# Moving x and the outputs of an eight-expert MLP into the weights' DMA queue

## The chip, the cores and the metric

The kernel runs on one core of a Trainium2 chip. A core has TensorE (PE) for matmuls with its weight load (PEld), VectorE (DVE), ScalarE (ACT), GpSimd (POOL) and SyncE (SP). Any of the last three may issue DMAs; all DMAs of the core run on the same 16 DMA engines. A DMA issued by POOL can change the type on its way, here fp32 in DRAM to bf16 on chip. Time is device microseconds (us), from the median of the runs; the profile is of one execution.

## What is computed

Eight experts, each a two-layer MLP with a ReLU between, and each on its own 256 rows:

```python
    n_experts, capacity, hidden, expert_hidden = 8, 256, 512, 2048
def reference(x, w1, w2):
    h = np.matmul(x, w1)
    h = np.maximum(h, 0)
    return np.matmul(h, w2).astype(np.float32)
```

All arrays are fp32 in DRAM. Each w1[e] and each w2[e] has 4.19 MB, each x[e] and each output 0.524 MB: 71.3 MB are read and 4.19 MB written. Inside, the kernel works in bf16 with fp32 sums.

## The kernel before

The kernel walks through the experts 0 to 7. Per expert it needs four things.

- **x.** `load_x` (line 57, issued by SP) brings x[e] as fp32 into one of three buffers. `prepare` casts it to bf16 on VectorE (line 88), transposes it in eight 128x128 blocks on TensorE (line 92) and copies the result from PSUM (line 94).
- **w1.** `load_w1` (line 62, POOL) is one DMA that casts 4.19 MB of fp32 to 2.1 MB of bf16; four buffers. Each of the 128 partitions gets one long row.
- **w2.** `load_w2` (line 75, POOL) does the same for w2, but in pieces for the last two experts: `PIECES` cuts the 16 k-rows of expert 6 into 8, 4, 4 and those of expert 7 into 4, 4, 3, 2, 1, 1, 1. Whole w2 have three buffers, pieces their own.
- **The matmuls.** `layer1` makes 64 matmuls (line 108) in eight pairs, each pair followed by a ReLU on ScalarE (line 115) into `hT`. `layer2` makes 32 (line 131); VectorE copies each half of the result to `out_sb` (line 142), except that ScalarE copies the last half of expert 7 (line 140).

POOL's DMAs run from one list, w1 and w2 of each expert in turn, except that w1 of expert 7 stands before w2 of expert 6. `advance` takes two loads from it per expert. Inside `manual_schedule`, PE and POOL execute in the order in which the code is written. On TensorE that is: first layer of e, transposes of e+1, second layer of e; at the end the first layer of 7 comes before the second layers of 6 and 7.

A load waits until its buffer is free (for TensorE), and, from the ninth POOL DMA on, also for the landing of the POOL DMA eight before it. DMAs of one queue are moved in the order of their issue.

Outputs of experts 0 to 4 are stored by SP (line 149). Those of experts 5 and 6 (`DEFER`) are stored by POOL after all weights (line 176). Expert 7's two halves are stored by SP and ACT as soon as each is copied (line 145).

Of the kernel before, what the change touches and what calls it, by code (L numbers as in the profile page):

```python
# [8 lines left out]

FP32 = mybir.dt.float32  # L10
BF16 = mybir.dt.bfloat16

@with_exitstack
def kernel(
    ctx: ExitStack,
    tc: tile.TileContext,  # L20
    x: bass.AP,
    w1: bass.AP,
    w2: bass.AP,
    out: bass.AP,
):
    nc = tc.nc
    P = 128
    E, C, H = x.shape
    F = w1.shape[2]
    MC = C // P  # L30
    K1 = H // P
    K2 = F // P

    x_v = x.rearrange("e (p mo) k -> e p (mo k)", mo=MC)
    out_v = out.rearrange("e (p mo) k -> e p (mo k)", mo=MC)
    w1_v = w1.rearrange("e (p ko) n -> e p (ko n)", ko=K1)
    w2_v = w2.rearrange("e (p j) n -> e p (j n)", p=P)

    const = ctx.enter_context(tc.tile_pool(name="const", bufs=1))
    x_pool = ctx.enter_context(tc.tile_pool(name="x_pool", bufs=3))  # L40
    xb_pool = ctx.enter_context(tc.tile_pool(name="xb_pool", bufs=2))
    xT_pool = ctx.enter_context(tc.tile_pool(name="xT_pool", bufs=2))
    w1_pool = ctx.enter_context(tc.tile_pool(name="w1_pool", bufs=4))
    w2_pool = ctx.enter_context(tc.tile_pool(name="w2_pool", bufs=4))
    hT_pool = ctx.enter_context(tc.tile_pool(name="hT_pool", bufs=2))
    out_pool = ctx.enter_context(tc.tile_pool(name="out_pool", bufs=4))
    psum_t = ctx.enter_context(tc.tile_pool(name="psum_t", bufs=1, space=bass.MemoryType.PSUM))
    psum_h = ctx.enter_context(tc.tile_pool(name="psum_h", bufs=3, space=bass.MemoryType.PSUM))
    psum_o = ctx.enter_context(tc.tile_pool(name="psum_o", bufs=4, space=bass.MemoryType.PSUM))

    identity = const.tile([P, P], BF16, name="identity")

    xs, w1s, w2s = {}, {}, {}

    def load_x(e):
        t = x_pool.tile([P, MC * H], FP32, name="x_sb")
        nc.sync.dma_start(t[:], x_v[e])
        xs[e] = t

    def load_w1(e):  # L60
        t = w1_pool.tile([P, K1 * F], BF16, name="w1_sb")
        nc.gpsimd.dma_start(t[:], w1_v[e])  # L62
        w1s[e] = t

    PIECES = {E - 2: [8, 4, 4], E - 1: [4, 4, 3, 2, 1, 1, 1]}
    BUFS = {16: 3, 8: 1, 4: 4, 3: 1, 2: 1, 1: 3}

    DEFER = (E - 3, E - 2)

    def load_w2(e):  # L70
        w2s[e] = []
        k = 0
        for n in PIECES.get(e, [16]):
            c = w2_pool.tile([P, n * H], BF16, name=f"w2_{n}", bufs=BUFS[n])
            nc.gpsimd.dma_start(c[:], w2_v[e, :, k * H:(k + n) * H])  # L75
            for q in range(n):
                w2s[e].append(c[:, q * H:(q + 1) * H])
            k += n


    weights = []
    for e in range(E):
        weights += [(load_w1, e), (load_w2, e)]
    weights[-3], weights[-2] = weights[-2], weights[-3]

    def prepare(e):
        xb = xb_pool.tile([P, MC, P, K1], BF16, name="xb")
        nc.vector.tensor_copy(xb[:].rearrange("p m q k -> p (m q k)"), xs[e][:])  # L88
        xt_ps = psum_t.tile([P, K1, MC, P], BF16, name="xt_ps")
        for ko in range(K1):  # L90
            for mo in range(MC):
                nc.tensor.transpose(xt_ps[:, ko, mo, :], xb[:, mo, :, ko], identity[:])  # L92
        xT = xT_pool.tile([P, K1, C], BF16, name="xT")
        nc.vector.tensor_copy(  # L94
            xT[:].rearrange("p k c -> p (k c)"),
            xt_ps[:].rearrange("p k m q -> p (k m q)"),
        )
        return xT

    def layer1(e, xT):  # L100
        w1_r = w1s[e][:].rearrange("p (ko q j) -> p ko q j", ko=K1, j=K2)
        hT = hT_pool.tile([P, K2, C], BF16, name="hT")
        for pr in range(K2 // 2):
            h_ps = psum_h.tile([P, 2, C], FP32, name="h_ps")
            for s in range(2):
                j = pr * 2 + s
                for ko in range(K1):
                    nc.tensor.matmul(  # L108
                        h_ps[:, s, :],
                        w1_r[:, ko, :, j],  # L110
                        xT[:, ko, :],
                        start=(ko == 0),
                        stop=(ko == K1 - 1),
                    )
            nc.scalar.activation(  # L115
                hT[:, pr * 2:pr * 2 + 2, :].rearrange("p a c -> p (a c)"),
                h_ps[:].rearrange("p a c -> p (a c)"),
                mybir.ActivationFunctionType.Relu,
            )
        return hT  # L120

    def layer2(e, hT):
        last = e == E - 1
        out_sb = out_pool.tile([P, MC, H], FP32, name="out_sb")
        o_ps = [psum_o.tile([P, H], FP32, name="o_ps") for _ in range(MC)]
        if e in PIECES:
            order = [(k, m) for k in range(K2) for m in range(MC)]
        else:
            order = [(k, m) for m in range(MC) for k in range(K2)]
        for k, m in order:  # L130
            nc.tensor.matmul(  # L131
                o_ps[m][:],
                hT[:, k, m * P:(m + 1) * P],
                w2s[e][k],
                start=(k == 0),
                stop=(k == K2 - 1),
            )
            if k == K2 - 1:
                if last and m == 1:
                    nc.scalar.copy(out_sb[:, m, :], o_ps[m][:])  # L140
                else:
                    nc.vector.tensor_copy(out_sb[:, m, :], o_ps[m][:])  # L142
                if last:
                    eng = nc.scalar if m == 1 else nc.sync
                    eng.dma_start(out_v[e, :, m * H:(m + 1) * H], out_sb[:, m, :])
        if e in DEFER:
            deferred.append((e, out_sb))
        elif not last:
            nc.sync.dma_start(out_v[e], out_sb[:].rearrange("p m h -> p (m h)"))

    deferred = []

    def advance(n):
        for _ in range(n):
            if weights:
                f, e = weights.pop(0)
                f(e)

    load_x(0)
    load_x(1)  # L160
    advance(1)
    make_identity(nc, identity)
    advance(1)
    with tc.manual_schedule(engines={mybir.EngineType.PE, mybir.EngineType.Pool}):
        xT = prepare(0)
        for e in range(E - 1):
            advance(2)
            if e + 2 < E:
                load_x(e + 2)
            hT = layer1(e, xT)  # L170
            xT = prepare(e + 1)
            if e == E - 2:
                hT_last = layer1(E - 1, xT)
            layer2(e, hT)
        for e, o in deferred:
            nc.gpsimd.dma_start(out_v[e], o[:].rearrange("p m h -> p (m h)"))  # L176
        layer2(E - 1, hT_last)


# [1 line left out]
_INS = ['x', 'w1', 'w2']  # L181
_OUTS = [((8, 256, 512), 'float32')]
# [25 lines left out]
```

## Time and profile before

| What | Value |
|---|---|
| Median of 8 runs | 184.11 us (183.69 to 185.18) |
| The profiled execution's own time | 184.12 us |
| Its span, first to last instruction | 182.3 us |
| TensorE matmuls, busy | 131.3 us (72%) |
| VectorE, ScalarE, busy | 21.0 us, 40.1 us |
| Matmuls of `layer1`, `layer2` | 71.3 us (311 ns each), 55.9 us (379 ns each) |
| Casts of x on VectorE | 5.6 us (8 x 701 ns) |
| w1 loads, issue to landing | 64.7 us median |
| x loads by SP, issue to landing | 27.8 us median |
| Stores by SP of experts 0 to 4, issue to landing | 25.4 us median |
| The two stores by POOL, issue to landing | 8.5 us median |
| Second of these issued | at 172.65 us |
| Expert 7's halves issued by SP and ACT | at 178.70 and 178.81 us |
| The same, issue to landing | 2.0 and 2.6 us |
| First POOL load issued | at 1.25 us |
| First matmul of `layer1` | at 16.45 us |

How to read it: the chain of work that ended last is followed back from the end, and gives for each step when it started, how long it took and what it was. A row of waits names who waited, for whom, the sum in us, how often and the longest. The slices cut the span in 40 equal parts; a digit is the busy share in tenths, 9 for 90% and more. A queue's row has its packets, the MB that they wrote and the time that they took as a share of 16 engines; packets can overlap, so shares may sum to more than 100%. A view by windows gives the same for any stretch of time.

### The profile page before, as it was taken

Reading aid. Unit: us, or ns where it says so; the run is one execution under the profiler, and the core shown is the slowest. Engines: PE = TensorE matmul, PEld = TensorE weight load, DVE = VectorE, ACT = ScalarE, POOL = GpSimd, SP = SyncE. Lnnn points to the kernel's source line nnn. Section 1 sums busy time; section 2 is a strip of 40 time slices with the busy share of each in tenths; the row PEclk is TensorE's granted clock in tenths of the full one; section 3 lists DMA queues with packets and bytes.
Section 4 is the critical chain, followed back from the end, with each engine's and each line's share of the span. In section 5 each row is a group of like instructions: output and inputs, shape, how many; then the busy total and the mean of one; then the engine's idle time right before and its main releaser. Section 6 shows DMA issues by size and latency. Waiting matters only on the chain.

```text
span 182.3 us, 1886 instructions
## 1 busy us (share of the span) xinstructions
PE 131.3 (72%) x824; PEld 92.3 (51%) x832; DVE 21.0 (12%) x31; ACT 40.1 (22%) x66; POOL 15.1 (8%) x32
## 2 busy tenths in 40 slices
PE   0203979539896496946989389595978679899990
PEld 0103874228842395415864069342874259794440
DVE  0301013100121002110031100211010200100201
ACT  2000550003600054001440026200450016461001
POOL 7300000200002000020030010101001010112100
PEclk9999999966999789995799969998799969999998
DMA  5999999999999999999999999999999998999993
GB/s 220 272 226 216 258 245 216 245 257 216 227 276 215 220 279 219 217 272 230 215 265 238 216 261 230 208 223 230 216 242 233 230 230 182 223 202 216 206 296 138
DMA packets 5911, 42.05 MB, mean 231 GB/s; under 512 B 656, under 2 KB 1040, under 8 KB 3984
## 3 DMA queue, kind: packets, MB, share of 16 engines
q0 software_dynamic: 3744, 34.60, 88.6%
q1 hardware_dynamic: 2016, 7.08, 10.3%
q10 hardware_dynamic: 144, 0.26, 0.4%
q8 instruction: 6, 0.10, 0.2%
q14 instruction: 1, 0.01, 0.0%
HBM read 71.30 MB, written 4.19 MB: 414 GB/s over the span
## 4 chain that ended last, share of the span: by engine, by line
PE 57%; DMA 26%; another core or an unknown queue 12%; POOL 1%; issue 1%; DVE 0%; ACT 0%; POOLq 0%
PE h_ps L108 29%; PE o_ps L131 27%; DMA w<-in_w_dram 26%; PE xt_ps L92 1%; POOL w_sb L62 1%; DVE xT L94 0%; ACT out_sb L140 0%; POOL w L75 0%; POOL identity masks.py:199 0%; POOL identity masks.py:197 0%; POOLq masks.py:199 0%; POOLq L192 0%
## 5 line engine op out<-in xcount | busy, mean ns | idle before, releaser
L108 PE MATMUL h_ps<-xT,w_sb 128*128 128x256 bf16 x512 | 71.3, 311 | 33.3 <-DMA w_sb<-in_w_dram 32.4
L108 PEld LDWEIGHTS <-w_sb 128*128 128x128 bf16 x512 | 63.2, 150 | 42.8 <-DMA w_sb<-in_w_dram 36.6
L115 ACT ACTIVATE hT<-h_ps 128x512 bf16<-128x512 f32 x64 | 38.2, 597 | 124.7 <-PE h_ps L108 124.7
L131 PE MATMUL o_ps<-w,hT 128*128 128x512 bf16 x248 | 55.9, 379 | 8.7 <-DMA w<-in_w_dram 8.3
L131 PEld LDWEIGHTS <-hT 128*128 128x128 bf16 x256 | 25.0, 98 | 37.6 <-issue 9.0
L75 POOL DMA_DIRECT2D w<-in_w_dram x16 | 8.5, 532 | 136.9 <-PE o_ps L131 71.7
L142 DVE COPY out_sb<-o_ps 128x512 f32<-128x512 f32 x15 | 10.3, 691 | 58.0 <-PE o_ps L131 58.0
L94 DVE COPY xT<-xt_ps 128x1024 bf16<-128x1024 bf16 x8 | 5.5, 692 | 84.1 <-PE xt_ps L92 84.1
L92 PE MATMUL xt_ps<-identity,xb 128*128 128x128 bf16 x64 | 5.3, 230 | 4.9 <-DVE xb L88 4.9
L88 DVE CAST xb<-x_sb 128x1024 bf16<-128x1024 f32 x8 | 5.6, 701 | 15.5 <-DMA x_sb<-in_x_dram 15.5
L92 PEld LDWEIGHTS <-xb 128*128 128x128 bf16 x64 | 4.7, 117 | 4.9 <-DVE xb L88 4.9
L62 POOL DMA_DIRECT2D w_sb<-in_w_dram x8 | 5.0, 630 | 13.5 <-PE h_ps L108 12.7
L140 ACT COPY out_sb<-o_ps 128x512 f32<-128x512 f32 x1 | 0.6, 586 | 13.2 <-PE o_ps L131 13.2
L176 POOL DMA_DIRECT2D out_dram<-out_sb x2 | 1.1, 536 | 7.3 <-DVE out_sb L142 5.1
L115 ACT ACT_TABLE_LOAD x1 | 1.3, 1283 | 0.7 <-PEq L192 0.7
masks.py:199 POOL TENSOR_SCALAR_AFFINE_SELECT identity<-identity 128x128 bf16<-128x128 bf16 x1 | 0.3, 315 | 0.1
masks.py:197 POOL MEMSET identity<- 128x128 bf16 x1 | 0.2, 224 | 0.0
L192 POOL MEMSET const-float32-0.0<- 128x1 f32 x1 | 0.1, 99 | 0.2 <-issue 0.2
L192 POOL MEMSET const-bfloat16-1.0<- 128x1 bf16 x1 | 0.1, 102 | 0.0
L192 POOL MEMSET const-uint8-127<- 128x1 uint8 x1 | 0.1, 102 | 0.0
L192 POOL MEMSET const-float32-1.0<- 128x1 f32 x1 | 0.1, 99 | 0.0
## 6 DMA issues: line engine op xcount, KB each, us to landing
w_sb<-in_w_dram POOLq DMA_DIRECT2D x8, 2048.0 KB, 64.7
w<-in_w_dram POOLq DMA_DIRECT2D x6, 2048.0 KB, 58.1
x_sb<-in_x_dram SPq DMA_DIRECT2D x8, 512.0 KB, 27.8
out_dram<-out_sb SPq DMA_DIRECT2D x5, 512.0 KB, 25.4
w<-in_w_dram POOLq DMA_DIRECT2D x4, 512.0 KB, 56.1
w<-in_w_dram POOLq DMA_DIRECT2D x1, 1024.0 KB, 67.3
out_dram<-out_sb POOLq DMA_DIRECT2D x2, 512.0 KB, 8.5
w<-in_w_dram POOLq DMA_DIRECT2D x1, 384.0 KB, 35.7
```

The source lines that it names most:

```text
L62: nc.gpsimd.dma_start(t[:], w1_v[e])
L75: nc.gpsimd.dma_start(c[:], w2_v[e, :, k * H:(k + n) * H])
L88: nc.vector.tensor_copy(xb[:].rearrange("p m q k -> p (m q k)"), xs[e][:])
L92: nc.tensor.transpose(xt_ps[:, ko, mo, :], xb[:, mo, :, ko], identity[:])
L94: nc.vector.tensor_copy(xT[:].rearrange("p k c -> p (k c)"), xt_ps[:].rearrange("p k m q -> p (k m q)"),)
L108: nc.tensor.matmul(h_ps[:, s, :], w1_r[:, ko, :, j], xT[:, ko, :], start=(ko == 0), stop=(ko == K1 - 1),)
L115: nc.scalar.activation(hT[:, pr * 2:pr * 2 + 2, :].rearrange("p a c -> p (a c)"), h_ps[:].rearrange("p a c -> p (a c)"), mybir.ActivationF ...
L131: nc.tensor.matmul(o_ps[m][:], hT[:, k, m * P:(m + 1) * P], w2s[e][k], start=(k == 0), stop=(k == K2 - 1),)
L140: nc.scalar.copy(out_sb[:, m, :], o_ps[m][:])
L142: nc.vector.tensor_copy(out_sb[:, m, :], o_ps[m][:])
L176: nc.gpsimd.dma_start(out_v[e], o[:].rearrange("p m h -> p (m h)"))
L192: nc = _bacc.Bacc("TRN2", target_bir_lowering=False, num_devices=1)
```

## The change

x of experts 2 to 7 is no longer loaded by SP and cast by VectorE. POOL loads it in pairs, (2, 3), (4, 5) and (6, 7), with the cast in the DMA, each pair placed in the weights' list before w1 of expert 1, 3 and 5. x of experts 0 and 1 is loaded and cast as before. Every load of w2 now fills a part of one whole buffer out of four. Expert 6's w2 comes in pieces of 8, 8 and expert 7's in 4, 4, 4, 2, 2.

Outputs are collected in one tile for each group: (0, 1, 2), (3, 4, 5, 6) and (7). POOL stores the first group in one DMA, which stands in its queue between w1 of expert 7 and w2 of expert 6, and the second group in one DMA after the last piece of w2. Expert 7's two halves are stored as before. The identity for the transposes is made twice.

The order of POOL's DMAs is then: w1 of 0, w2 of 0, x of 2 and 3, w1 and w2 of 1, w1 and w2 of 2, x of 4 and 5, w1 and w2 of 3 and of 4, x of 6 and 7, w1 and w2 of 5, w1 of 6, w1 of 7, outputs 0 to 2, w2 of 6 (2 pieces), w2 of 7 (5 pieces), outputs 3 to 6. The rule of eight counts all of these. TensorE's order is the one of before. SP keeps x of 0 and 1 and one half of expert 7.

```diff
-    x_pool = ctx.enter_context(tc.tile_pool(name="x_pool", bufs=3))
+    x_pool = ctx.enter_context(tc.tile_pool(name="x_pool", bufs=2))
-    out_pool = ctx.enter_context(tc.tile_pool(name="out_pool", bufs=4))
+    out_pool = ctx.enter_context(tc.tile_pool(name="out_pool", bufs=1))
...
+    PIECES = {E - 2: [8, 8], E - 1: [4, 4, 4, 2, 2]}
+    GROUPS = [(0, 1, 2), (3, 4, 5, 6), (7,)]
+    GROUP = {e: g for g in GROUPS for e in g}
+    DEFER = GROUPS[-2]
+    X_GROUPS = [(2, 3), (4, 5), (6, 7)]
...
+    def load_x(g):
+        t = xb_pool.tile([P, 2, MC, P, K1], BF16, name="xb2")
+        nc.gpsimd.dma_start(
+            t[:].rearrange("p e m q k -> p e (m q k)"), xg_v[:, g[0]:g[0] + 2, :]
+        )
+        for i, e in enumerate(g):
+            xbs[e] = t[:, i]
...
     def load_w2(e):
-        w2s[e] = []
+        w2s[e] = t = w2_pool.tile([P, K2 * H], BF16, name="w2_sb")
         k = 0
-        for n in PIECES.get(e, [16]):
-            c = w2_pool.tile([P, n * H], BF16, name=f"w2_{n}", bufs=BUFS[n])
-            nc.gpsimd.dma_start(c[:], w2_v[e, :, k * H:(k + n) * H])
...
+        for n in PIECES.get(e, [K2]):
+            nc.gpsimd.dma_start(t[:, k * H:(k + n) * H], w2_v[e, :, k * H:(k + n) * H])
             k += n
+    def store(g):
+        nc.gpsimd.dma_start(
+            og_v[:, g[0]:g[-1] + 1, :], outs[g][:].rearrange("p e m h -> p e (m h)")
+        )
...
     def prepare(e):
-        xb = xb_pool.tile([P, MC, P, K1], BF16, name="xb")
-        nc.vector.tensor_copy(xb[:].rearrange("p m q k -> p (m q k)"), xs[e][:])
+        xb = xbs[e]
...
     def layer2(e, hT):
-        out_sb = out_pool.tile([P, MC, H], FP32, name="out_sb")
+        g = GROUP[e]
+        if e == g[0]:
+            outs[g] = out_pool.tile([P, len(g), MC, H], FP32, name=f"out_sb{g[0]}")
+        out_sb = outs[g][:, e - g[0]]
...
-        if e in DEFER:
-            deferred.append((e, out_sb))
-        elif not last:
-            nc.sync.dma_start(out_v[e], out_sb[:].rearrange("p m h -> p (m h)"))
...
+    load_x_first(0)
+    load_x_first(1)
     with tc.manual_schedule(engines={mybir.EngineType.PE, mybir.EngineType.Pool}):
+        f, e = loads.pop(0)
+        f(e)
+        make_identity(nc, identity)
+        f, e = loads.pop(0)
+        f(e)
+        make_identity(nc, identity)
+        issue([(load_w2, 0), (load_x, X_GROUPS[0]), (load_w1, 1), (load_w2, 1), (load_w1, 2)])
         xT = prepare(0)
         for e in range(E - 1):
-            advance(2)
-            if e + 2 < E:
-                load_x(e + 2)
+            issue(
+                [(load_w2, e + 2), (load_w1, e + 3), (load_w1, E - 1), (load_w2, e + 1)]
+                + [(load_x, g) for g in X_GROUPS if g[0] <= e + 4]
+            )
+            for g in GROUPS[:-2]:
+                if g[-1] == e - 1:
+                    store(g)
             hT = layer1(e, xT)
             xT = prepare(e + 1)
             if e == E - 2:
                 hT_last = layer1(E - 1, xT)
             layer2(e, hT)
-        for e, o in deferred:
-            nc.gpsimd.dma_start(out_v[e], o[:].rearrange("p m h -> p (m h)"))
+        store(DEFER)
         layer2(E - 1, hT_last)
```

## The prediction

> **What bounds the kernel now.** I read the slices first, then the queues, then the waits on the matrix engine, then the chain, and last the DMA load in stretches of my choice. The slices and queues of the whole execution:
>
> ```profile
> DMA  5999999999999999999999999999999998999993
> q0 software_dynamic: 3744, 34.60, 88.6%
> q1 hardware_dynamic: 2016, 7.08, 10.3%
> ```
>
> The 16 DMA engines are busy from the first slice to the last. POOL's queue (q0) takes 88.6% of them and SP's (q1) 10.3%. The MB are bytes written: a weight is read as fp32 and written as bf16, so q0's weights cost twice their MB in reads. The waits agree:
>
> ```profile
> PE h_ps L108 <- DMA w_sb<-in_w_dram: 32.4, 7, 10.5
> PE o_ps L131 <- DMA w<-in_w_dram: 8.3, 6, 2.0
> ```
>
> TensorE waits 32.4 us for w1 and 8.3 us for w2. POOL's long waits for buffers (71.7 us) cost nothing, since a full 2 MB load lands a median 58 to 65 us after its issue: some five loads are always queued. The chain's steps late in the span:
>
> ```profile
> 61.60 8.87 PE h_ps L108 x64
> 83.62 9.78 PE h_ps L108 x64
> 105.67 8.87 PE h_ps L108 x64
> 147.00 8.84 PE h_ps L108 x64
> 157.16 7.19 PE h_ps L108 x64
> 164.61 10.74 PE o_ps L131 x49
> 175.40 2.77 PE o_ps L131 x12
> 178.19 0.59 ACT out_sb L140
> ```
>
> First layers start every 22.03 us while SP's queue is busy, which is the DMA's pace, and from 157 us TensorE runs almost without a gap to 178.17. The end is therefore balanced: DMA and TensorE finish about together. Five stretches of the view by windows (columns: stretch, length, then PE, PEld, DVE, ACT, POOL busy, clock, DMA share, GB/s) show the tail:
>
> ```profile
> 173.00:175.00 2.00, 2.00 (x11) 0.91 (x10) 0.00 (x0) 0.00 (x0) 0.19 (x1) 1.00 1.21 218
> 175.00:178.00 3.00, 2.95 (x14) 1.25 (x13) 0.02 (x1) 0.00 (x0) 0.00 (x0) 1.00 0.91 334
> 178.00:179.00 1.00, 0.16 (x1) 0.00 (x0) 0.67 (x1) 0.59 (x1) 0.00 (x0) 1.00 0.15 61
> 179.00:180.00 1.00, 0.00 (x0) 0.00 (x0) 0.00 (x0) 0.00 (x0) 0.00 (x0) 1.00 0.46 176
> 180.00:181.00 1.00, 0.00 (x0) 0.00 (x0) 0.00 (x0) 0.00 (x0) 0.00 (x0) 1.00 0.94 348
> ```
>
> The last weights end at about 175.3 (the rate turns from that of bf16 weights to that of fp32 stores, single microseconds give 226, 360, 412). The two deferred stores' data end at about 178.5 on the slowest engines (0.06 MB move after 178.0). Then the DMA lies nearly idle until expert 7's two halves move, 179.5 to 181.0. Data ends at 181.0, the span at 182.3.
>
> **Prices, from the DMA view of single stretches.** Between 20 and 110 us both queues run, between 140 and 155 only weights:
>
> ```profile
> q0 software_dynamic: 1174, 17.14, 89.2%
> q1 hardware_dynamic: 1154, 4.20, 12.3%
> ...
> q0 software_dynamic: 215, 3.18, 99.4%
> ...
> q0 software_dynamic: 389, 0.44, 120.6%
> ...
> q0 software_dynamic: 50, 0.20, 99.4%
> ```
>
> Weights alone: 3.18 x 2 / 15 us = 0.424 MB read per us. Beside SP's queue, 17.14 x 2 / 0.424 = 80.9 us of the 90 belong to weights, so SP's 4.20 MB cost 9.1 us: 1.14 us for a 0.524 MB x or store. The chain gives another price: 22.03 us is two weights and two SP transfers, and the 41.33 us from 105.67 to 147.00 are four weights and two SP transfers (the stores of experts 3 and 4), which makes 9.65 us a weight and 1.36 us an SP transfer. I take 1.2 us, nearer the longer average. The third row (173 to 175 us) is the last w2 pieces, most of its packets 1 KB long: 0.44 x 2 / 2 = 0.44 MB read per us, so casting short rows is no slower than long ones. The fourth (176.5 to 177) is stores alone in POOL's queue: 0.20 / 0.5 = 0.41 MB/us, 1.28 us per 0.524 MB store.
>
> **The change part by part**, on the DMA's account up to the last weight.
> 1. Six x (3.15 MB) and five stores (experts 0 to 4) leave SP's queue: 11 x 1.2 = 13.2 us removed (12.5 to 15.0 by the two prices).
> 2. The six x come back as three casting DMAs in POOL's queue, 4 KB read and 2 KB written per row. No such row is in the trace. Below: 1.20 us for 0.524 MB, the rate of the last pieces. Above: 1.38 us, what a 4 KB packet occupied an engine in SP's queue (12.3% of 90 us x 16 engines, over some 1,026 data packets, is 173 ns; eight per engine). I take 1.24, the rate of weights, which are the same kind of transfer: +7.4 us (7.2 to 8.3).
> 3. The store of experts 0 to 2 goes into the queue after w1 of 7: 3 x 1.28 = +3.8 us.
> 4. w2 of experts 6 and 7 is cut into 7 pieces, not 10: at most some tenths; I take -0.2 us.
> Sum: 7.4 + 3.8 - 13.2 - 0.2 = -2.2 us; the last weights end at 173.1.
> 5. Behind them stand four stores (experts 3 to 6), 5.1 us, where there were two, 2.6: +2.55 us.
> 6. Expert 7's two stores (0.52 MB, 1.28 us at 0.41) no longer wait for an idle DMA to start but join stores still moving.
> End of data: 178.5 - 2.2 + 2.55 + 1.28 = 180.1, against 181.0: -0.9 us.
>
> **What hides the rest.** Six casts on VectorE (701 ns each) vanish and the identity is made twice (0.22 + 0.32 us on POOL). Both hide behind TensorE's wait for the first weight until 16.4 us; uncovered, the second identity would cost 0.5 us. The order on TensorE is the same.
>
> POOL's queue gets new waits. x of 6 and 7 waits for the transposes of expert 3, about 68 us, and w1 of expert 5 to 7 and all later loads stand behind it. Loads up to w2 of 4 are queued by then, which last to about 107 us: 39 us of cover. The store of 0 to 2 waits for expert 2's copies (about 75 us) and an earlier load (about 90), with w2 of 6 and 7 behind it; their turn at the DMA comes after 150. Its buffer is its own.
>
> TensorE's tail: w2 of 7 needs 10 us, so w2 of 6 is in at 163.1 plus some 0.8 us of slow engines, 163.9. Its last 16 matmuls take 16 x 0.219 (10.74 us over 49) = 3.5 us, to 167.4. w2 of 7 is then consumed as it lands; after the last piece (two rows, 173.1 + 0.8) come four matmuls (0.9 us) and a copy (0.7 us), 175.5. The halves are issued then and move about 0.8 us later (178.70 to 179.5 now), near 176.5, while the four stores (173.1 to 178.2) move: TensorE has 1.5 to 2 us to spare.
>
> **A rule that speaks against it.** The Trainium skill, "DMA: Bandwidth & Descriptors", section "Anatomy of one DMA", gives a POOL-issued DMA about 2.0 us of fixed time, mostly the receipt of its last byte. The row here: the second deferred store was issued at 172.65 and landed 6.3 us later, 178.95, with data ending at 178.5, so 0.45 us; expert 7's last half landed at 178.8 + 2.6 = 181.4, 0.4 us after its data. By the row the end moves with the data (-0.9 us). By the rule, if POOL's store lands last, 2.0 - 0.4 = 1.6 us are added, and the sum is +0.7. I follow the row.
>
> **The sum.** The profiled execution took 184.12 us, its span 182.3. The span becomes 181.4, the time 183.2. The median shown is 184.11, so the same figure stands against it. About 0.3% (0.55 us) is what a measurement can tell here.
>
> **The rivals.**
> A. Nothing measurable. It is the same bytes through the same engines. With SP's traffic at 1.14 us a transfer and the cast at 1.38: 8.3 + 3.8 - 12.5 - 0.2 = -0.6, so +0.7; halfway between this and mine is 184.0. For it: the mixed stretch reads 0.428 MB/us against 0.424 alone, so interleaving already hid a little. Against: the rate of the short pieces.
> B. A larger gain. With 1.36 us removed and casts at 1.20: 7.2 + 3.8 - 15.0 - 0.2 = -4.2, so -2.9 us, 181.2; halfway, 182.2.
> C. Slower: the four-expert store comes too late. It cannot be issued before expert 6 is copied: 167.4 + 2 x 0.69 = 168.9, and its data should start at 173.1: cover 4.2 us. The first weight load was issued at 1.25, and q0's first packets appear after 4 us: up to 3.3 us from issue to data, for 128 rows. This store has 512. Past 4.2 us every microsecond is an idle DMA; at 6 us the gain of 0.9 turns into a loss of 0.9 (185.0). For it: nothing in the trace shows a DMA of so many rows. Against: POOL's issue instruction takes 530 to 550 ns for rows of 1 KB and of 16 KB alike, and the first packets may only have waited for x.
> That the change does nothing of what it says is excluded: SP's queue keeps only three DMAs.
>
> **Chances.** Mine (-0.9 us) 0.50, A 0.25, B 0.08, C 0.17. Part of A lies over the bound (0.03). Faster 0.57, same 0.22, slower 0.21. The range reaches to B's halfway point and to C at 6 us: 182.2 to 185.0. Mine alone: 182.6 to 183.7.
>
> **What would show it.** q1 down to about 1.3 MB (two x and one half); no slice of the DMA under 9 from the second to the last but one; first layers about 19.8 us apart where no x pair lies between, 22.3 where one does; first layer of expert 7 at about 150 to 152; the last weights at 173, the big store issued near 169; no idle stretch between stores and the last halves; data over at 180.1. Wrong would be a gap before the big store, x pairs costing over 2.8 us, or weights ending after 174.

## The result and the profile after

The changed kernel takes 182.48 us (median of 12 runs, 182.23 to 183.73) against 184.03 for the kernel before: ratio 0.9917, 95% interval 0.9897 to 0.9936. Timed again later on another chip it gave 0.9926 (0.9911 to 0.9941). That is 1.2 to 1.5 us faster, where 0.9 was forecast. The profiled execution took 182.48 us with a span of 180.7, against 184.12 and 182.3.

The slices and queues of the changed kernel, whole execution:

```profile
DMA  6999999999999989999999999899999989999994
q0 software_dynamic: 4768, 38.80, 97.6%
q1 hardware_dynamic: 432, 1.31, 2.0%
```

The DMA engines are as busy as before, but nearly all in POOL's queue. TensorE still waits for the same things as long:

```profile
PE h_ps L135 <- DMA w_sb<-in_w_dram: 34.3, 8, 9.3
PE o_ps L161 <- DMA w_sb<-in_w_dram: 8.4, 8, 2.4
```

The bound did not change. The end did. Windows of the changed kernel (columns as before: stretch, length, PE, PEld, DVE, ACT, POOL busy, clock, DMA share, GB/s):

```profile
171.00:172.00 1.00, 0.89 (x4) 0.47 (x5) 0.00 (x0) 0.00 (x0) 0.00 (x0) 1.00 1.12 260
172.00:173.00 1.00, 1.00 (x6) 0.41 (x6) 0.00 (x0) 0.00 (x0) 0.00 (x0) 1.00 1.03 348
173.00:174.00 1.00, 1.00 (x6) 0.49 (x5) 0.00 (x0) 0.00 (x0) 0.00 (x0) 1.00 1.07 434
...
177.00:178.00 1.00, 0.00 (x0) 0.00 (x0) 0.00 (x0) 0.00 (x0) 0.00 (x0) 1.00 0.99 389
178.00:179.00 1.00, 0.00 (x0) 0.00 (x0) 0.00 (x0) 0.00 (x0) 0.00 (x0) 0.82 0.37 143
179.00:180.00 1.00, 0.00 (x0) 0.00 (x0) 0.00 (x0) 0.00 (x0) 0.00 (x0) 0.50 0.09 35
```

The rate passes 348 GB/s in the microsecond from 172; before it passed 360 in the one from 175. So the last weights end about 3 us earlier; the last piece of w2 landed at 173.59 in place of 176.42. The DMA stays at 0.98 or more until 178, while it was nearly idle from 178 to 179.5 before. Data is over at about 179.5 in place of 181.0.

### The profile page after: what moved, and what is told of

The parts are those of the page before. It is cut to its first block, busy times and chain, and to the rows that moved or that the text cites. A ratio compares the mean times of both kernels' runs of the same rounds, so it can differ in the third digit from the quotient of the medians.

```text
span 180.7 us, 1853 instructions
## 1 busy us (share of the span) xinstructions
PE 126.7 (70%) x824; PEld 89.6 (50%) x832; DVE 17.1 (9%) x25; ACT 40.1 (22%) x66; POOL 16.4 (9%) x34
## 3 DMA queue, kind: packets, MB, share of 16 engines
q1 hardware_dynamic: 432, 1.31, 2.0%
HBM read 71.30 MB, written 4.19 MB: 418 GB/s over the span
## 4 chain that ended last, share of the span: by engine, by line
DMA 71%; another core or an unknown queue 11%; PE 10%; POOL 2%; issue 2%; ACT 0%; POOLq 0%
DMA w_sb<-in_w_dram 46%; DMA xb<-in_x_dram 25%; PE o_ps L161 6%; PE h_ps L135 4%; POOL w_sb L82 1%; POOL w_sb L88 1%; POOL xb L74 0%; ACT out_sb L170 0%; POOL identity masks.py:199 0%; POOL identity masks.py:197 0%; PE xt_ps L119 0%; POOLq masks.py:199 0%; POOLq L88 0%; POOLq L215 0%
## 5 line engine op out<-in xcount | busy, mean ns | idle before, releaser
L135 PE MATMUL h_ps<-xT,w_sb 128*128 128x256 bf16 x512 | 66.2, 297 | 34.3 <-DMA w_sb<-in_w_dram 34.3
L135 PEld LDWEIGHTS <-w_sb 128*128 128x128 bf16 x512 | 60.5, 148 | 41.6 <-DMA w_sb<-in_w_dram 37.7
L161 PE MATMUL o_ps<-w_sb,hT 128*128 128x512 bf16 x248 | 56.3, 379 | 8.9 <-DMA w_sb<-in_w_dram 8.4
L88 POOL DMA_DIRECT2D w_sb<-in_w_dram x13 | 7.0, 537 | 76.9 <-DMA w_sb<-in_w_dram 75.1
L82 POOL DMA_DIRECT2D w_sb<-in_w_dram x8 | 4.7, 587 | 31.3 <-PE h_ps L135 18.2
L74 POOL DMA_DIRECT2D xb<-in_x_dram x3 | 2.2, 718 | 26.4 <-PE xt_ps L119 26.4
L69 DVE CAST xb<-x_sb 128x1024 bf16<-128x1024 f32 x2 | 1.4, 695 | 4.6 <-DMA x_sb<-in_x_dram 4.6
```

Of the source, the lines that this page charges most:

```text
L69: nc.vector.tensor_copy(b[:].rearrange("p m q k -> p (m q k)"), t[:])
L74: nc.gpsimd.dma_start(t[:].rearrange("p e m q k -> p e (m q k)"), xg_v[:, g[0]:g[0] + 2, :])
L82: nc.gpsimd.dma_start(w1s[e][:], w1_v[e])
L88: nc.gpsimd.dma_start(t[:, k * H:(k + n) * H], w2_v[e, :, k * H:(k + n) * H])
L135: nc.tensor.matmul(h_ps[:, s, :], w1_r[:, ko, :, j], xT[:, ko, :], start=(ko == 0), stop=(ko == K1 - 1),)
L161: nc.tensor.matmul(o_ps[m][:], hT[:, k, m * P:(m + 1) * P], w2s[e][:, k * H:(k + 1) * H], start=(k == 0), stop=(k == K2 - 1),)
```

## The experiments

Theory 1, the one of the prediction: the total work of the DMA engines sets the end, and most of the gain is that stores fill the time in which the DMA waited for expert 7's halves. Theory 2: the landing of the last weights sets the end through TensorE. Theory 3: x is what pays, by the cheaper queue or without VectorE's casts.

### x alone

```diff
 # in the kernel before
...
     for e in range(E):
+        for g in X_GROUPS:
+            if g[0] == e + 1:
+                weights.append((load_x_pair, g))
         weights += [(load_w1, e), (load_w2, e)]
...
             advance(2)
-            if e + 2 < E:
-                load_x(e + 2)
```

> Before, with only x of experts 2 to 7 moved into POOL's queue as three casting pairs; stores and pieces as before. Theory 1 (the DMA engines' total work sets the end; most of the gain is that stores fill the idle DMA stretch ahead of expert 7's halves): six transfers at 1.24 us in place of six at about 1.3 us beside weights, so -0.4 us against before, 183.6 us, with the idle stretch near 179 us still there. Theory 3 (the gain is x itself: no VectorE cast, a cheaper queue): nearly all of the -1.5 us, 182.5 us.

Measured: 184.09 us, ratio 0.9996 (0.9976 to 1.0015). Theory 3 falls: moving x changes nothing in the kernel's time that can be measured. In the profiled executions the DMA did gain the 0.4 us that theory 1 gave it: the last half landed at 181.00, not 181.39. But both spans end at 182.3. SP closes the program with a list of waits for DMAs, 0.06 us each once the DMA is in. With x alone the DMA that lands last is the second of nine in that list; in the kernel before it is the last but one. The idle stretch is still there:

```profile
178.00:179.00 1.00, 0.00 (x0) 0.00 (x0) 0.28 (x1) 0.39 (x1) 0.00 (x0) 1.00 0.09 37
179.00:180.00 1.00, 0.00 (x0) 0.00 (x0) 0.00 (x0) 0.00 (x0) 0.00 (x0) 1.00 0.87 326
180.00:181.00 1.00, 0.00 (x0) 0.00 (x0) 0.00 (x0) 0.00 (x0) 0.00 (x0) 0.74 0.52 199
```

### Everything but x

```diff
 # in the changed kernel
-        for g in X_GROUPS:
-            if g[0] == e + 1:
-                loads.append((load_x, g))
...
     def prepare(e):
-        xb = xbs[e]
+        xb = xb_pool.tile([P, MC, P, K1], BF16, name="xb")
+        nc.vector.tensor_copy(xb[:].rearrange("p m q k -> p (m q k)"), xs[e][:])
...
+            if e + 2 < E:
+                load_x_first(e + 2)
```

> The changed kernel with x back in SP's queue as fp32 and cast by VectorE; grouped stores and pieces as changed. Theory 1: +0.4 us against the changed kernel, 182.9 us, no idle stretch at the end. Theory 3: the gain is lost, 184.0 us.

Measured: 182.81 us, ratio 0.9929 (0.9901 to 0.9957), the time that theory 1 had. Nearly the whole gain is there without x, and no idle stretch:

```profile
177.00:178.00 1.00, 0.00 (x0) 0.00 (x0) 0.00 (x0) 0.00 (x0) 0.00 (x0) 1.00 1.03 406
178.00:179.00 1.00, 0.00 (x0) 0.00 (x0) 0.00 (x0) 0.00 (x0) 0.00 (x0) 1.00 0.47 178
```

That theory 1's 0.4 us came out is in part luck: in the profiled executions the last half landed at 179.81, in the changed kernel at 179.84. The span is 0.4 us longer only behind that, where SP has six more waits to go through. This kernel also gives the cleanest price of an SP transfer. Its first layers in order of time (start, length, instructions, idle before):

```profile
39.34 8.87 PE L131 MATMUL h_ps<-xT,w_sb 128*128 128x256 bf16 x64 [4.70 <-DMA w_sb<-in_w_dram]
61.39 10.06 PE L131 MATMUL h_ps<-xT,w_sb 128*128 128x256 bf16 x64 [3.97 <-DMA w_sb<-in_w_dram]
...
101.52 8.80 PE L131 MATMUL h_ps<-xT,w_sb 128*128 128x256 bf16 x64 [2.59 <-DMA w_sb<-in_w_dram]
120.94 8.88 PE L131 MATMUL h_ps<-xT,w_sb 128*128 128x256 bf16 x64 [2.67 <-DMA w_sb<-in_w_dram]
```

With two x of SP between two first layers the step is 22.05 us; with none, 19.42. An SP transfer of 0.524 MB costs 1.31 us, a weight 9.71. In the changed kernel the same rows give the pair of x:

```profile
57.45 7.21 PE L135 MATMUL h_ps<-xT,w_sb 128*128 128x256 bf16 x64 [2.68 <-DMA w_sb<-in_w_dram]
...
79.26 9.03 PE L135 MATMUL h_ps<-xT,w_sb 128*128 128x256 bf16 x64 [5.10 <-DMA w_sb<-in_w_dram]
```

21.81 less 19.42 is 2.39 us for two x, 1.20 each. Six times 0.11 is 0.7 us of the DMA's time at most; the last landings show 0.4 us of it with x alone and none here.

### Only two experts behind the last weights

```diff
-    GROUPS = [(0, 1, 2), (3, 4, 5, 6), (7,)]
+    GROUPS = [(0, 1, 2), (3, 4), (5, 6), (7,)]
...
+            if e == E - 3:
+                store(GROUPS[1])
...
-            for g in GROUPS[:-2]:
+            for g in GROUPS[:1]:
```

> The changed kernel with only experts 5 and 6 stored behind the last weights; 3 and 4 are stored in POOL's queue between w2 of 6 and w2 of 7. Theory 1: last weights 2.5 us later (about 174.8), TensorE and expert 7's halves 2.5 us later too, the two stores' data over before the halves start, so an idle stretch of about 1 us returns: +0.9 us against the changed kernel, 183.4 us. Theory 2 (the landing of the last weights sets the end through TensorE): the full +2.5 us, 185.0 us.

Measured: 183.42 us, ratio 0.9959 (0.9938 to 0.9979). Some 0.7 us of the gain are lost, near the 0.9 of theory 1; theory 2 wanted 2.5. About 0.25 us of the loss lie outside the profiled span: the time less the span is 2.0 us in every run of this kernel, 1.7 to 1.8 in those of the changed one. The profile is of this kernel's fastest run (183.03 us). The hole before expert 7's halves, issued at 177.40 and 177.51, is back:

```profile
176.00:177.00 1.00, 0.86 (x4) 0.20 (x2) 0.32 (x1) 0.10 (x1) 0.00 (x0) 1.00 0.78 320
177.00:178.00 1.00, 0.00 (x0) 0.00 (x0) 0.37 (x1) 0.48 (x1) 0.00 (x0) 1.00 0.26 107
178.00:179.00 1.00, 0.00 (x0) 0.00 (x0) 0.00 (x0) 0.00 (x0) 0.00 (x0) 1.00 0.75 285
```

### All seven behind the last weights

```diff
-            for g in GROUPS[:-2]:
-                if g[-1] == e - 1:
-                    store(g)
...
+        store(GROUPS[0])
         store(DEFER)
```

> The changed kernel with the store of experts 0 to 2 moved behind the last weights as well. Theory 1: the same bytes, the DMA engines are busy to the end either way: 182.4 us, within 0.3 us of the changed kernel, though the last weights land 3.7 us earlier (about 168.5). Theory 2: -3.7 us, 178.8 us.

Measured: 182.86 us, ratio 0.9933 (0.9908 to 0.9958). TensorE ends 4 us earlier (the halves are issued at 171.15, not 175.21), and nothing is won; the time is even 0.4 us above theory 1's. Theory 2 falls here. Data even ends a little earlier, at 179.1; yet the span is 181.2, not 180.7:

```profile
177.00:178.00 1.00, 0.00 (x0) 0.00 (x0) 0.00 (x0) 0.00 (x0) 0.00 (x0) 0.50 0.86 336
178.00:179.00 1.00, 0.00 (x0) 0.00 (x0) 0.00 (x0) 0.00 (x0) 0.00 (x0) 0.50 0.27 111
179.00:180.00 1.00, 0.00 (x0) 0.00 (x0) 0.00 (x0) 0.00 (x0) 0.00 (x0) 0.50 0.00 0
```

From the end of data to the end of the span this kernel takes 2.2 us, the changed one 1.2. The instruction with which POOL closes the program shows why, here first and then in the changed kernel (shortest, median and longest in ns, then first and last start):

```profile
L224 POOLq DRAIN  x3: 45/88/15412, 165.1 to 181.0; - x3
...
L226 POOLq DRAIN  x3: 45/88/11007, 168.7 to 180.4; - x3
```

The longest one starts after POOL's last issue and ends at 180.5 here and at 179.7 in the changed kernel, both times 1.1 us after POOL's last store has landed (179.39 and 178.57). In the changed kernel ACT's half lands later anyway, at 179.84; here nothing else is left to wait for.

### The deferral alone

```diff
 # in the kernel before
-    DEFER = (E - 3, E - 2)
+    DEFER = (E - 5, E - 4, E - 3, E - 2)
-    out_pool = ctx.enter_context(tc.tile_pool(name="out_pool", bufs=4))
+    out_pool = ctx.enter_context(tc.tile_pool(name="out_pool", bufs=5))
```

> Before, with one thing changed: experts 3 and 4 are also stored by POOL behind the last weights, so four single stores stand there (out_pool has five buffers for it). x, pieces and the stores of 0 to 2 as before. Theory 1: two SP transfers of 1.3 us leave the weights' time, two stores of 1.28 us come behind them, and expert 7's halves no longer wait for an idle DMA: -1.0 us, 183.1 us. Theory 2 (the last weights' landing sets the end): -2.6 us, 181.5 us. A theory in which the deferral needs the moved x or the emptied SP queue: no gain, 184.1 us.

Measured: 182.98 us, beside 183.72 for the kernel before on that chip: ratio 0.9950 (0.9935 to 0.9965), that is 0.9 us, near theory 1's 1.0. One line and one buffer bring more than half of the gain, with neither x moved nor SP's queue emptied.

```profile
175.00:176.00 1.00, 0.00 (x1) 0.00 (x0) 0.51 (x1) 0.58 (x1) 0.00 (x0) 1.00 1.02 418
176.00:177.00 1.00, 0.00 (x0) 0.00 (x0) 0.00 (x0) 0.00 (x0) 0.00 (x0) 1.00 1.06 434
177.00:178.00 1.00, 0.00 (x0) 0.00 (x0) 0.00 (x0) 0.00 (x0) 0.00 (x0) 1.00 1.00 397
```

The DMA is full while VectorE and ScalarE copy the last result, and after it.

### The big store by SP

```diff
-        store(DEFER)
+        nc.sync.dma_start(
+            og_v[:, DEFER[0]:DEFER[-1] + 1, :],
+            outs[DEFER][:].rearrange("p e m h -> p e (m h)"))
```

> The changed kernel with the store of experts 3 to 6 issued by SP, not by POOL, at the same place in the code: it no longer stands behind the last weights but shares the DMA engines with them from about 169.5 us. Theory 1 as refined (place in the queue matters because it keeps stores for the time in which TensorE finishes): last weights about 1.5 to 2 us later, expert 7's halves issued about 177, an idle stretch of some 1 us before them: +0.7 us against the changed kernel, 183.2 us. Theory that the place in the queue is irrelevant and only the amount of work counts: 182.5 us.

Measured: 182.67 us, ratio 0.9937 (0.9920 to 0.9955), near the figure for "irrelevant" and 0.5 us under mine. The mechanism shows; its price does not:

```profile
174.00:175.00 1.00, 0.05 (x1) 0.05 (x1) 0.00 (x0) 0.00 (x0) 0.00 (x0) 1.00 1.00 408
175.00:176.00 1.00, 0.97 (x4) 0.24 (x3) 0.21 (x1) 0.00 (x0) 0.00 (x0) 1.00 1.05 434
176.00:177.00 1.00, 0.00 (x0) 0.00 (x0) 0.48 (x1) 0.59 (x1) 0.00 (x0) 1.00 0.85 348
177.00:178.00 1.00, 0.00 (x0) 0.00 (x0) 0.00 (x0) 0.00 (x0) 0.00 (x0) 1.00 0.80 311
```

TensorE stands still from 174 to 175 for the last piece, and the halves are issued at 176.51, 1.3 us later than in the changed kernel. But the DMA drops only to 0.80 and 0.85. TensorE had that much time to spare.

### The pieces and the grouping

```diff
 # old pieces, in the changed kernel
-    PIECES = {E - 2: [8, 8], E - 1: [4, 4, 4, 2, 2]}
+    PIECES = {E - 2: [8, 4, 4], E - 1: [4, 4, 3, 2, 1, 1, 1]}
```

> The changed kernel with the old cut of w2: 8, 4, 4 for expert 6 and 4, 4, 3, 2, 1, 1, 1 for expert 7. Theory 1: the ten pieces take about 0.27 us more of the DMA engines than the seven (their landings span 20.0 us before, 19.7 after): +0.25 us, 182.75 us. Theory 2: the smaller last piece lets TensorE end 0.2 to 0.4 us earlier, 182.2 us.

Measured: ratio 0.9955 (0.9940 to 0.9970), 182.96 us. Against the changed kernel's 0.9926 on a chip with nearly the same time before (183.75 against 183.72) that is 0.4 to 0.5 us slower. It is not theory 1's reason, though. The median span is 180.8 us in the runs of both, and the time less the span is 2.16 to 2.25 us with the old pieces, 1.76 to 1.82 in the changed kernel. The difference lies outside the span, and its cause stays open. Neither theory shows in the span; in the kernel before, with four stores deferred, the new pieces brought the last landing of w2 forward by 0.15 us.

```diff
 # single stores, in the changed kernel
     def store(g):
...
+        for i, e in enumerate(g):
+            nc.gpsimd.dma_start(out_v[e], outs[g][:, i].rearrange("p m h -> p (m h)"))
```

> The changed kernel with each expert of a group stored by a DMA of its own, in the same places of POOL's queue. Theory 1: the same work, 182.5 us within 0.3 us. A theory in which the gain comes from grouping (fewer DMAs, longer ones): half a microsecond or more is lost, 183.0 us or above.

Measured: 183.19 us, ratio 0.9957 (0.9937 to 0.9977). As the changed kernel had been timed on another chip, it was run again beside this one:

> The changed kernel once more, beside the two next ones on one chip, since the variants of the last two groups were each timed on another chip than it. Theory 1: ratio to before 0.991 to 0.994.

> The changed kernel with single stores, as before in e9, now beside the changed kernel. Theory 1: the same as the changed kernel within 0.3 us. Grouping theory: 0.5 us or more slower than it.

Measured: the changed kernel 182.56 us, 0.9926 (0.9911 to 0.9941); single stores 182.93 us, 0.9948 (0.9928 to 0.9969), with runs from 182.53 to 183.67. The intervals overlap, and the median differs by 0.4 us, between the two expectations. The spans do not differ: their medians are 180.75 us with single stores and 180.8 in the changed kernel. The time less the span is 2.09 to 2.21 us in all 18 runs with single stores, 1.76 to 1.82 in the changed kernel beside them. So grouping changes nothing that the span holds. In both profiles of single stores, and in no other, a packet of instructions is fetched 1.5 us after the last instruction (queues from 180 us on; the span ends at 180.4):

```profile
q14 instruction: 1, 0.01, 0.6%
```

Whether it is the cause is not shown; the old pieces cost as much outside the span without one.

The last one joins the deferral and the pieces in the kernel before:

```diff
 # in the kernel of "The deferral alone"
-    PIECES = {E - 2: [8, 4, 4], E - 1: [4, 4, 3, 2, 1, 1, 1]}
-    BUFS = {16: 3, 8: 1, 4: 4, 3: 1, 2: 1, 1: 3}
+    PIECES = {E - 2: [8, 8], E - 1: [4, 4, 4, 2, 2]}
+    BUFS = {16: 3, 8: 2, 4: 3, 2: 2}
```

> Before with four single stores behind the last weights and the new cut of w2 (8, 8 and 4, 4, 4, 2, 2), x and the stores of 0 to 2 by SP as before. Theory 1: -0.9 us from the stores and -0.25 us from the pieces, ratio 0.994, within 0.4 us of the changed kernel. If x and the first three stores in POOL's queue matter, it stays 0.5 us or more behind the changed kernel.

Measured: 182.84 us, ratio 0.9943 (0.9928 to 0.9958). That is 0.9 of the 1.2 us that the whole change gave on that chip, with x and three stores still on SP: 0.3 us behind the changed kernel, as theory 1 had it. No version was clearly faster than the changed kernel.

## Why the prediction was right

Its mechanism held, and the gain came out larger because terms up to the last weight were mis-sized. Landings in the profiled executions, in us, show it part by part:

| Kernel | Last piece of w2 | Last store by POOL | Last half of expert 7 | End of span |
|---|---|---|---|---|
| Before | 176.42 | 178.95 | 181.39 | 182.3 |
| x alone | 176.25 | 178.82 | 181.00 | 182.3 |
| The deferral alone | 173.76 | 178.78 | 180.03 | 181.1 |
| The deferral and the pieces | 173.61 | 178.64 | 179.91 | 181.0 |
| Changed | 173.59 | 178.57 | 179.84 | 180.7 |
| All seven deferred | 169.34 | 179.39 | 178.38 | 181.2 |

The deferral and the pieces together land their last DMA within 0.1 us of the changed kernel. The moved x and the moved first three stores add nothing there that shows.

**The bound.** "DMA and TensorE finish about together": deferring all seven stores let TensorE finish 4 us earlier and won nothing, so of the two the DMA is the one that counts once its end is filled.

**Step 1, SP's traffic removed: mis-sized.** I took 1.2 us a transfer, between 1.14 from the queues' MB and 1.36 from the chain. Measured 1.31, from steps between first layers of one kernel. The MB of a stretch were the poorer source: they fix the price as a small difference between two large amounts, and 0.424 MB/us, from 15 us, was too low a rate. A weight of 4.19 MB every 9.71 us is 0.432, and with that the same row gives 1.33. Over 11 transfers it is 1.2 us more taken away.

**Step 2, the casting pairs.** 1.24 us an x forecast, 1.20 measured; the slow end, 1.38, is excluded. Short rows cast as fast as long ones.

**Steps 3 and 4.** The store of three cost more than 3.8 us: from the landing of w1 of 6 to that of the first piece of w2 of 6 it is 18.94 us with it and 14.58 without it (all seven deferred), so 4.4. The pieces gave 0.15 us where 0.2 was forecast. Priced anew, the steps give 7.2 + 4.4 - 14.4 - 0.15 = -3.0 us; the last weights landed 2.8 us earlier, and 2.2 was forecast. The two mis-sized terms pulled in opposite directions.

**Step 5.** Two more stores behind the weights, +2.55 us forecast. From the last piece of w2 to POOL's last store it is 5.0 us, before 2.5: +2.45.

**Step 6, expert 7's halves join.** They were issued at 175.2, as forecast (175.5), and the last landed 1.3 us after POOL's store, where it was 2.4 before: the idle stretch was worth 1.2 us, as forecast (2.5 less 1.28). With the deferral alone it is gone too (1.25 us from POOL's store to the last half). The first half moved at 176.49, as forecast (176.5), but 1.3 us after its issue and not 0.8. The queues of the changed kernel from 175 to 176, 176.5 to 177, and 178 to 179:

```profile
q0 software_dynamic: 107, 0.44, 106.3%
...
q0 software_dynamic: 35, 0.11, 52.7%
q1 hardware_dynamic: 42, 0.09, 44.1%
...
q10 hardware_dynamic: 41, 0.07, 18.7%
q1 hardware_dynamic: 37, 0.06, 16.6%
q0 software_dynamic: 5, 0.01, 2.2%
```

Until 176 only POOL's store moves; from 176.5 on SP's and ACT's share the engines with it. For the total this made no difference that shows.

**End of data**: 180.1 forecast, 179.5 measured. The 0.6 us are those of the last weights.

**Signs.** Three slices of the DMA show an 8 where none under 9 was forecast, and first layers stood 19.4 and 21.8 us apart, not 19.8 and 22.3. The end of data came 0.6 us early. The other signs came about as written.

**The cover.** The big store was issued at 168.70 (forecast 168.9, where the sum gives 168.8), and no microsecond from 170 to 178 shows a share under 0.98. So its 512 rows were ready within the 3.5 us until the last weights ended, and rival C did not occur. How much of that time they need was not measured. TensorE's spare time was between 1.3 us, which the SP store used up at next to no cost, and 2.2 us, with which the hole came back (halves issued at 177.40); 1.5 to 2 was forecast.

**The rule weighed against the row.** If about 2 us of fixed time came after the data of the last POOL DMA, the sum would have been +0.7. It was not; but in the changed kernel ACT's half lands last. Where POOL's store lands last (all seven deferred), it landed 0.3 us after its data (179.1), as the row has it, not 2. The span is longer there by 1.0 us after the data, but that is POOL's closing instruction.

**Rivals A and B.** The measured 1.2 to 1.5 us lie between my figure and B's halfway point (1.9), for B's reason, a dearer SP transfer, less what the store of three cost on top.

## What to carry to other kernels

In a DMA-bound kernel, look at the tail for a stretch in which the queues are empty while the last result is computed and copied, and put stores that are already complete behind the last load: here two more stores of 1.25 us were enough, and seven were no better than four. Take the price of a transfer that shares the engines from the step between two repeats of the loop with and without it, not from megabytes in a window. Moving bytes from one queue to another without taking any away is worth little by itself: here 0.4 us of the DMA's time and none of the kernel's. Before a difference of some tenths is explained by what the data did, compare when the last DMA landed, when the span ended and what the time holds beyond it.

## What was not expected

Kernels whose last DMA lands at the same time still differ in time by some tenths, from three parts behind it: how many of SP's closing waits are left, POOL's closing instruction, and what the time holds beyond the span. The last part is 1.7 to 1.9 us in most kernels here, 2.0 with only two experts deferred and 2.1 to 2.25 with single stores or the old pieces, nearly the same in every run of a kernel. What sets it stays open.

SP's first packet of the last stores moved at 176.49, 1.3 us after its issue at 175.21, while POOL's store ran; in the kernel before, with the DMA idle, it took 0.8 us. With all seven stores behind the weights it took 3.8 us (171.15 to 174.96), and then SP's and ACT's halves moved beside POOL's store for almost 3 us. In the middle of the kernel before, SP's 4.20 MB moved beside POOL's 17.14 in 90 us. What sets this delay was not taken apart.
